# Cross attention in a hybrid layer kernel: the second value product moves ahead of the first operands of w_xo, and two w_xo products move between the heads

## The chip, the cores and the metric

The kernel runs on one core of one Trainium2 chip. The metric is the device time of one execution in microseconds. Five engines work side by side, each through its own queue of instructions in the order in which they were written there: TensorE (PE in the profile; its weight loads are PEld), VectorE (DVE), ScalarE (ACT), GpSimd (POOL) and SyncE (SP), which here only issues the transfers from main memory. An instruction that waits for another engine holds up everything behind it in its own queue.

## The reference, cut to what matters

One layer over 1024 rows of width 1024: a mixer (state space model and causal attention), then a cross attention to 256 memory rows, then a squared-ReLU MLP, each followed by a residual and a layer norm. The change touches the cross attention alone:

```python
def memory_cross_attention(h, mem, w_xq, w_xk, w_xv, w_xo):
    q = (h @ w_xq).reshape(bsz, seq, XATTN_HEADS, XATTN_HEAD_DIM)
    k = (mem @ w_xk).reshape(bsz, m, XATTN_HEADS, XATTN_HEAD_DIM)
    v = (mem @ w_xv).reshape(bsz, m, XATTN_HEADS, XATTN_HEAD_DIM)
    s = jnp.einsum('bshd,bmhd->bhsm', q, k).astype(jnp.float32) * (XATTN_HEAD_DIM ** -0.5)
    p = jax.nn.softmax(s, axis=-1).astype(v.dtype)
    o = jnp.einsum('bhsm,bmhd->bshd', p, v).reshape(bsz, seq, D_MODEL)
    return o @ w_xo
...
h = layer_norm(DN_ALPHA * h + xa, ln2_g[l], ln2_b[l])
```

## The kernel before

**Three matmuls for one.** Operands are split into a rounded high part and a low remainder, and `mm3` (lines 150 to 152) adds hi·hi, hi·lo and lo·hi into one PSUM bank. So each operand costs, ahead of its matmuls, a cast on ACT (the high part) and a subtraction (the low part), most of them on POOL. For weights that is `split_w` (load on SP, cast at line 120, subtraction at line 122). There are four single PSUM banks (names b...) and two double ones (names bb...), taken in turn; a new use of a bank waits until the last use has been read.

**Products of 1024 by 1024** go by Strassen's scheme (`strassen`): seven products, each 48 matmuls of 512 columns on PE, in an order given by a string; for w_xo it is `XOO = '3657142'`. The operands of a product are made by `op_split`: a sum of two quarters takes a copy into a double bank on ACT (line 367), a sum on DVE (line 371), the cast on ACT (line 373) and the subtraction on POOL or DVE (line 375); a single quarter takes the cast on ACT (line 361) and the subtraction on POOL (line 362). `chain` yields such work step by step: each `next` prepares one product's operands or runs one product. The results are added into the residual rows by DVE (line 1192).

**The cross attention** works in eight units: a unit is one half of the rows (hf) and one head (hd), in the order `xu`: (0,0), (0,1), (1,0), (1,1), then the same with heads 2 and 3. A list of short steps, `STEPS`, written by hand, sets their order:

- `k` n: the key product of head n, with two weight tiles of w_xk
- `v` n: the value product, columns 512·n to 512·n+511 of w_xv (two heads), 48 matmuls; `v1` serves heads 2 and 3, units 4 to 7. Four weight tiles go through `split_w`; the two banks are then split into the value tile (cast at line 1357 on ACT, subtraction at line 1358 on DVE)
- `s` n: split of the query of unit n (ACT line 1378, then DVE line 1379), 24 matmuls of 256 columns, row maxima (DVE line 1394), exponentials (ACT line 1397), reciprocals (DVE line 1398) and scaling (POOL line 1401)
- `t` n: eight transposes of the probabilities on PE (line 1409), then the split (ACT line 1411, DVE line 1412)
- `o` n: the value times the probabilities, 12 matmuls of 512 columns; the copies out are line 1422, on ACT and on DVE
- `r`: one of eight residual tiles (ACT line 279, DVE lines 280 and 281)
- `c`: one `next` of the w_xo chain. Product 3 needs units 0, 1 and its weights; product 6 units 0 to 3; product 5 units 0, 1, 4, 5; products 7, 1, 4 and 2 all or some of units 4 to 7

The steps only fix the priority; a scheduler lays the instructions out on each engine's queue in about that order, and the steps of `c` that remain after the list are taken by `norm_between` at line 1504 (13 less the number of `c` in the list). The order on the queues is then fixed in the program.

Of the kernel before, what the change touches and what calls it, by code (L numbers as in the profile page):

```python
# [510 lines left out]
def body(tc, ctx, a, dbg=None):  # L511
# [107 lines left out]
    s5 = k_.slot()  # L619
# [84 lines left out]
    t4 = k_.slot().rearrange("p (g s h) -> p g s h", s=8, h=16)  # L704
# [163 lines left out]
    s4 = [v4(z)[:, :, 0:15, 0:7] for z in sct]  # L868
# [9 lines left out]
    for q in range(2):  # L878
        for two in range(2):
            b = k_.bank()  # L880
            r0 = two * 64
# [475 lines left out]
            A.copy(hi.bitcast(FR), bs[i][:, 0:512])  # L1357
            V.tensor_sub(lo.bitcast(FR), bs[i][:, 0:512], hi)

    STEPS = "k0 s0 k1 s1 t0 r0 v0 r0 t1 o0 s2 r0 k2 o1 r0 s3 t2 r0 k3 o2 r0 t3 s4 r0 o3 c0 r0 v1 t4 s5 o4 s6 c0 t5 o5 c0 t6 s7 o6 c0 t7 o7".split()  # L1360
    steps = [(z[0], int(z[1])) for z in STEPS]

    xq, h1 = {}, {}
# [228 lines left out]
```

## Time and profile before

| | |
|---|---|
| median of 3 runs | 1653.34 us (1650.19 to 1653.36) |
| the profiled execution | 1652.23 us |
| its span, first to last instruction | 1650.4 us |
| mean granted TensorE clock | 0.981 |
| PE busy | 1539.5 us, 93% of the span |
| DVE, POOL, ACT busy | 1243.3, 988.0, 976.5 us (75%, 60%, 59%) |
| the chain that ended last | PE 71%, DVE 15%, ACT 7%, POOL 3%, issue 3% |
| transfers | 71 GB/s mean; queue q1 20.5% of 16 engines |

A row of the timeline has the start, the duration, engine, source line, operation, output and input names, and in brackets the idle time of the engine ahead of it with what ended it. A matmul's duration in a row runs on past the start of the next one, since matmuls are pipelined; the pitch from start to start is what one costs in a row of many. The cross attention from its third transpose on to the fourth w_xo product is the stretch from 844 to 944 us.

### The profile page before, as it was taken

How to read it: one execution, taken by the hardware profiler on the slowest of the kernel's cores; microseconds unless marked ns; L12 is line 12 of the kernel's file. 1: busy time of each engine (PE TensorE's matmuls, PEld its weight loads, DVE VectorE, ACT ScalarE, POOL GpSimd, SP SyncE). 2: the span in 40 equal slices, each digit the busy share in tenths (PEclk: the TensorE clock that was granted, in tenths of full speed). 3: DMA queues.
4: the chain of work that ended last, by engine and by line, in shares of the span. 5: the costliest groups of instructions: out<-in, count | busy, mean ns of one | idle time of the engine just before them, and what ended most of it. 6: DMA issues, size and time to landing. Idle time of an engine off the chain costs nothing.

```text
span 1650.4 us, 20758 instructions
## 1 busy us (share of the span) xinstructions
PE 1539.5 (93%) x7480; PEld 1263.0 (77%) x7480; DVE 1243.3 (75%) x1977; ACT 976.5 (59%) x1415; POOL 988.0 (60%) x538
## 2 busy tenths in 40 slices
PE   6979999999989999999977899899999999999995
PEld 4867778778768778778866687678888888888884
DVE  7970926767777969956574686999598949876998
ACT  5632235666678537684573647766866766667661
POOL 3223243664547767665563554676878767878776
PEclk9989999999999999999998899999999999999998
DMA  6212121111052541103220120022111302021102
GB/s 240 81 39 71 53 71 56 59 60 50 15 177 81 201 154 51 52 0 129 102 102 1 32 86 37 28 75 64 39 51 52 102 1 77 26 103 50 57 22 102
DMA packets 40107, 117.61 MB, mean 71 GB/s; under 512 B 4804, under 2 KB 6340, under 8 KB 40004
## 3 DMA queue, kind: packets, MB, share of 16 engines
q1 hardware_dynamic: 40004, 116.29, 20.5%
q8 instruction: 59, 0.97, 0.2%
q14 instruction: 44, 0.36, 0.1%
HBM read 98.90 MB, written 16.78 MB: 70 GB/s over the span
## 4 chain that ended last, share of the span: by engine, by line
PE 71%; DVE 15%; ACT 7%; POOL 3%; issue 3%; DMA 1%; SPq 0%; POOLq 0%; ACTq 0%; DVEq 0%
PE b L151 20%; PE b L150 20%; PE b L152 20%; DVE sx L1192 1%; PE bb L1034 1%; PE b L1071 1%; DVE c L182 1%; DVE t L371 1%; PE bb L1037 1%; DVE sx L1223 1%; ACT bb L367 1%; PE bb L1038 1%; PE b L1090 1%; DVE sx L224 1%; DVE sa L1249 1%
## 5 line engine op out<-in xcount | busy, mean ns | idle before, releaser
L151 PE MATMUL b<-sw,sa 128*128 128x512 f32 (+3 forms) x1504 | 579.6, 385 | 12.8 <-POOL sw L375 6.7
L150 PE MATMUL b<-sw,sa 128*128 128x512 f32 (+3 forms) x1504 | 578.6, 385 | 12.8 <-ACT sw L120 5.4
L152 PE MATMUL b<-sw,sa 128*128 128x512 f32 (+3 forms) x1504 | 577.7, 384 | 2.7 <-POOL sa L375 2.2
L151 PEld LDWEIGHTS b<-sw,sa 128*128 128x128 f32 x1504 | 284.7, 189 | 71.8 <-POOL sw L375 10.3
L150 PEld LDWEIGHTS b<-sw,sa 128*128 128x128 f32 x1504 | 284.5, 189 | 69.2 <-ACT sw L120 5.7
L152 PEld LDWEIGHTS b<-sw,sa 128*128 128x128 f32 x1504 | 284.5, 189 | 57.9 <-POOL sa L375 4.0
L375 POOL TENSOR_TENSOR sa<-t,sa 128x1024 fp32r<-128x1024 f32 x105 | 257.6, 2469 | 118.8 <-ACT sa L373 106.9
L367 ACT COPY bb<-sa 128x1024 f32<-128x1024 f32 x230 | 233.1, 1018 | 135.8 <-DVE t L371 69.1
L1192 DVE TENSOR_TENSOR sx<-sx,b 128x512 f32<-128x512 f32 x288 | 185.1, 675 | 35.2 <-PE b L152 35.0
L375 POOL TENSOR_TENSOR sw<-t,sw 128x1024 fp32r<-128x1024 f32 x73 | 180.9, 2484 | 43.4 <-ACT sw L373 34.2
L371 DVE TENSOR_TENSOR t<-bb,sa 128x1024 f32<-128x1024 f32 x119 | 144.1, 1217 | 35.1 <-ACT bb L367 18.9
L1249 DVE TENSOR_TENSOR sa<-sa,b 128x512 f32<-128x512 f32 x192 | 124.9, 678 | 46.8 <-ACT sa L1247 33.7
L373 ACT CAST sa<-t 128x1024 fp32r<-128x1024 f32 x105 | 109.1, 1049 | 59.3 <-DVE t L371 58.9
L362 POOL TENSOR_TENSOR sa<-sa,sa 128x1024 fp32r<-128x1024 f32 x36 | 90.2, 2519 | 57.8 <-ACT sa L361 34.2
L122 POOL TENSOR_TENSOR sw<-sraw,sw 128x1024 fp32r<-128x1024 f32 (+4 forms) x28 | 61.9, 2219 | 87.4 <-ACT sw L120 81.8
L150 PE MATMUL b<-sa,sw 128*128 128x512 f32 (+1 forms) x272 | 101.5, 373 | 3.3 <-DVE sa L1249 3.3
L152 PE MATMUL b<-sa,sw 128*128 128x512 f32 (+1 forms) x272 | 99.2, 365 | 0.0
L151 PE MATMUL b<-sa,sw 128*128 128x512 f32 (+1 forms) x272 | 99.2, 365 | 0.0
L362 POOL TENSOR_TENSOR sw<-sa,sw 128x1024 fp32r<-128x1024 f32 x32 | 81.1, 2550 | 27.9 <-ACT sw L361 27.9
L371 DVE TENSOR_TENSOR t<-bb,sraw 128x1024 f32<-128x1024 f32 x53 | 64.2, 1217 | 33.8 <-POOL sw L375 17.8
L373 ACT CAST sw<-t 128x1024 fp32r<-128x1024 f32 x73 | 76.2, 1052 | 15.3 <-PE b L151 7.6
L375 DVE TENSOR_TENSOR sw<-bb,sw 128x1024 fp32r<-128x1024 f32 x47 | 57.2, 1217 | 5.6 <-ACT sw L373 5.5
(341 smaller groups left out, 2792.5 us busy)
## 6 DMA issues: line engine op xcount, KB each, us to landing
sa<-in_w_up_dram SPq DMA_DIRECT2D x24, 512.0 KB, 4.0
sa<-in_w_dn_dram SPq DMA_DIRECT2D x24, 512.0 KB, 4.3
sx<-in_x_dram SPq DMA_DIRECT2D x16, 512.0 KB, 5.8
d_h<-t SPq DMA_DIRECT2D x16, 256.0 KB, 2.3
sraw<-in_w_gs_dram SPq DMA_DIRECT2D x8, 512.0 KB, 3.2
d_gs<-t SPq DMA_DIRECT2D x16, 256.0 KB, 2.9
t<-d_gs SPq DMA_DIRECT2D x16, 256.0 KB, 2.8
d_ms<-t SPq DMA_DIRECT2D x16, 256.0 KB, 2.1
```

Source lines behind the costliest of these rows:

```text
L122: (nc.vector if self.rawtag == "a" and self.nsw % SWV == 0 else nc.gpsimd).tensor_sub(lo[:, :cols].bitcast(FR), raw[:, :cols], hi[:, :cols])
L150: mm(out, A[0].bitcast(FR), B[0].bitcast(FR), start=start, stop=False)
L151: mm(out, A[0].bitcast(FR), B[1].bitcast(FR), start=False, stop=False)
L152: mm(out, A[1].bitcast(FR), B[0].bitcast(FR), start=False, stop=stop)
L182: self.nc.vector.bn_stats(st[:, h, :], x[:, h * 512:(h + 1) * 512])
L362: (GP if z is x[c] else V).tensor_sub(H[c][1].bitcast(FR), z, H[c][0])
L367: A.copy(P[c], x[c])
L371: V.tensor_tensor(T[c], P[c], y[c], op=op)
L373: A.copy(H[c][0].bitcast(FR), T[c])
L375: (V if T[c] is P[c] else GP).tensor_sub(H[c][1].bitcast(FR), T[c], H[c][0])
L1192: V.tensor_tensor(v, v, b, op=op)
L1249: V.tensor_tensor(z[:, s_], z[:, s_], b, op=op)
```

## The change

One string changes: `v1`, one `r`, the `c` steps and some `t` and `s` steps stand in another order, and there are five `c` in the list where there were four.

```diff
-    STEPS = "k0 s0 k1 s1 t0 r0 v0 r0 t1 o0 s2 r0 k2 o1 r0 s3 t2 r0 k3 o2 r0 t3 s4 r0 o3 c0 r0 v1 t4 s5 o4 s6 c0 t5 o5 c0 t6 s7 o6 c0 t7 o7".split()
+    STEPS = "k0 s0 k1 s1 t0 r0 v0 r0 t1 o0 s2 r0 k2 o1 r0 s3 t2 r0 k3 o2 r0 t3 v1 r0 s4 o3 r0 c0 s5 t4 c0 s6 o4 c0 t5 s7 o5 c0 t6 t7 c0 o6 o7".split()
```

The same work is done: the same products, splits, transfers and sums. Up to `t3` the two programs are alike on all engines.

**ACT, from the operands of w_xo's product 3 on to the casts of v1's weights, before.** Names: sa and sw are SBUF tiles (sw the weights' halves), bb a double bank, t a sum. The two L120 rows are the last two weight tiles of `v1`; L1378 is the query of unit 5; the rows to the second L373 are product 3's operands.

```order
L367 COPY bb1518_8069<-sa1504_8045 128x1024
L361 CAST sa1510_8057<-sa1440_7656 128x1024
L367 COPY bb1519_8071<-sa1505_8047 128x1024
L361 CAST sa1512_8059<-sa1461_7790 128x1024
L373 CAST sw1514_8065<-t1520_8073 128x1024
L373 CAST sw1516_8067<-t1521_8075 128x1024
L279 COPY bb1522_8081<-sx1083_5852 128x1024
L1411 CAST sa1532_8156<-b1531_8151 128x512
L1411 CAST sa1534_8164<-b1533_8159 128x512
L120 CAST sw1525_8099<-sa1527_8101 128x1024
L1378 ACTIVATE sa1535_8167<-sa1261_6739 128x1024
L120 CAST sw1528_8117<-sa1530_8119 128x1024
```

The ACT queue of the changed kernel, from the split behind `t3` (the row L1411) on, at the place where those casts stand now; L1378 sa1502 is the query of unit 4, and the two L1357 rows split the finished `v1` banks.

```order
L1411 CAST sa1492_7976<-b1491_7971 128x512
L1378 ACTIVATE sa1502_8049<-sa1257_6707 128x1024
L120 CAST sw1495_7981<-sa1497_7983 128x1024
L120 CAST sw1498_7999<-sa1500_8001 128x1024
L1357 CAST sa1417_7554<-b1493_7979 128x512
L1357 CAST sa1419_7556<-b1494_7980 128x512
L1397 ACTIVATE sa1504_8053,c1506_8067<-bb1505_8054,c1506_8067 128x256 x2
L279 COPY bb1512_8111<-sx1083_5852 128x1024
L1397 ACTIVATE sa1504_8053,c1508_8087<-bb1507_8074,c1508_8087 128x256 x2
```

The two casts of `v1`'s weights stand ahead of unit 4's softmax now; before they stood behind it and behind all of product 3's operands. The split of `v1`'s result has moved up with them.

**ACT, further on in the changed kernel,** from the copy out of `o3` (L1422) on to the split of `t4`'s transposes (the two L1411); the L367, L361 and L373 rows are product 3's operands, L1378 sa1531 the query of unit 5, the two L1397 rows its exponentials.

```order
L1422 COPY sa1509_8094<-b1510_8095 128x512
L367 COPY bb1527_8139<-sa1513_8115 128x1024
L361 CAST sa1519_8127<-sa1440_7656 128x1024
L367 COPY bb1528_8141<-sa1514_8117 128x1024
L361 CAST sa1521_8129<-sa1461_7790 128x1024
L373 CAST sw1523_8135<-t1529_8143 128x1024
L373 CAST sw1525_8137<-t1530_8145 128x1024
L1378 ACTIVATE sa1531_8151<-sa1261_6739 128x1024
L1397 ACTIVATE sa1533_8155,c1535_8169<-bb1534_8156,c1535_8169 128x256 x2
L1411 CAST sa1539_8201<-b1538_8196 128x512
L1397 ACTIVATE sa1533_8155,c1537_8189<-bb1536_8176,c1537_8189 128x256 x2
L1411 CAST sa1541_8209<-b1540_8204 128x512
```

Before, L1378 of unit 5 and the split of `t4` (the L1411 rows) stood behind product 3's operands as well; but between `t4` and unit 5's scores PE had the second half of `v1`. Now `v1` is done by then, and the split of `t4` stands behind L1378 and between the exponentials of unit 5.

**PE, the transposes of the last units, before:** the names ending in 8503 and 8511 are the banks of `t7`, 8520 and 8528 those of `o7`.

```order
L1409 MATMUL b1605_8503<-cst_58,sa1584_8418 128x128
L1409 MATMUL b1607_8511<-cst_58,sa1584_8418 128x128
L150 MATMUL b1610_8520<-sa1606_8508,sa1417_7554 128x512
L150 MATMUL b1611_8528<-sa1606_8508,sa1417_7554 128x512
L151 MATMUL b1610_8520<-sa1606_8508,sa1417_7554 128x512
```

PE at that place in the changed kernel: 8470 and 8478 are the banks of `t6`, 8486 and 8494 those of `t7`, 8502 the first bank of w_xo's product 6.

```order
L1409 MATMUL b1598_8470<-cst_58,sa1559_8247 128x128 x4
L1409 MATMUL b1600_8478<-cst_58,sa1559_8247 128x128 x4
L1409 MATMUL b1602_8486<-cst_58,sa1577_8385 128x128 x2
L1409 MATMUL b1604_8494<-cst_58,sa1577_8385 128x128 x2
L1409 MATMUL b1602_8486<-cst_58,sa1577_8385 128x128
L1409 MATMUL b1604_8494<-cst_58,sa1577_8385 128x128
L1409 MATMUL b1602_8486<-cst_58,sa1577_8385 128x128
L1409 MATMUL b1604_8494<-cst_58,sa1577_8385 128x128
L150 MATMUL b1606_8502<-sw1549_8227,sa1542_8212 128x512
L151 MATMUL b1606_8502<-sw1550_8228,sa1542_8212 128x512
L152 MATMUL b1606_8502<-sw1549_8227,sa1543_8213 128x512
```

The 48 matmuls of product 6 now stand ahead of both `o6` and `o7`, and `t6` and `t7` stand together and take all four single banks; b1606 is the bank that b1598 had.

On SP the loads of `v1`'s last two weight tiles move ahead of four loads of w_xo. The two come into tiles that the scores of unit 3 free (before: into tiles that the split of `t3` and unit 4's scores free).

## Rows read from the trace of the kernel before

**Rows 1.** The page: TensorE's busy time with its share of the span, and the clock granted to it in 40 equal slices of 41.3 us (in tenths of full speed; 21 and 22 are the slices from 866 to 949 us).

```profile
PE 1539.5 (93%) x7480; PEld 1263.0 (77%) x7480; DVE 1243.3 (75%) x1977; ACT 976.5 (59%) x1415; POOL 988.0 (60%) x538
PEclk9989999999999999999998899999999999999998
```

**Rows 2.** Busy time by stage. Columns: the stretch and its length, then for PE, PEld, DVE, ACT and POOL the busy us with the number of instructions, then the granted clock as a share of full speed, the transfers' share and GB/s. The first is the whole stretch that the change reorders, the next three are parts of it, the last lies behind it.

```profile
844.45:943.46 99.01, 73.26 (x333) 57.85 (x333) 55.77 (x69) 53.77 (x88) 46.15 (x33) 0.84 0.12 42
857.90:876.90 19.00, 9.18 (x25) 6.83 (x26) 6.84 (x7) 7.86 (x10) 13.09 (x6) 0.64 0.00 0
887.30:899.70 12.40, 5.04 (x13) 3.57 (x14) 7.97 (x10) 10.85 (x19) 7.65 (x7) 0.72 0.00 0
922.60:932.60 10.00, 5.65 (x12) 4.01 (x13) 5.17 (x6) 7.36 (x10) 2.65 (x2) 0.51 0.00 1
943.70:996.00 52.30, 52.30 (x236) 43.12 (x235) 44.38 (x82) 26.66 (x33) 28.57 (x13) 1.00 0.24 81
```

**Rows 3.** The timeline of PE: the end of `t4`'s transposes, the first matmuls behind the long waits (of `v1`'s second half twice, of `o5`, of `o7`), and the first matmul of w_xo's product 5.

```profile
856.85 1.03 PE L1409 MATMUL b<-cst,sa 128*128 128x128 f32 x8
863.33 1.22 PE L150 MATMUL b<-sw,sa 128*128 128x512 f32 x2 [5.44 <-ACT sw L120]
868.94 0.79 PE L151 MATMUL b<-sw,sa 128*128 128x512 f32 x1 [4.39 <-POOL sw L122]
894.27 1.22 PE L150 MATMUL b<-sa,sa 128*128 128x512 f32 x2 [7.07 <-ACT sa L1411]
926.55 1.22 PE L150 MATMUL b<-sa,sa 128*128 128x512 f32 x2 [4.00 <-ACT sa L1411]
943.68 0.39 PE L150 MATMUL b<-sw,sa 128*128 128x512 f32 x1
```

**Rows 4.** The timeline of PE, pitches: first and last of 24 matmuls of 512 columns (`v1`'s first half), of 12 in `v1`'s second half, and of 24 of 256 columns (unit 5's scores).

```profile
851.40 0.39 PE L150 MATMUL b<-sw,sa 128*128 128x512 f32 x1
856.62 0.39 PE L152 MATMUL b<-sw,sa 128*128 128x512 f32 x1
...
869.96 0.63 PE L150 MATMUL b<-sw,sa 128*128 128x512 f32 x1
874.65 0.53 PE L150 MATMUL b<-sw,sa 128*128 128x512 f32 x1
...
876.84 0.28 PE L150 MATMUL bb<-sa,sa 128*128 128x256 f32 x1
879.59 0.28 PE L152 MATMUL bb<-sa,sa 128*128 128x256 f32 x1
```

**Rows 5.** The loads of `v1`'s last two weight tiles: their issue on the SP queue; their size and median us from issue to landing in the list of transfers from 830 to 1000 us; and, of the timeline of PE, the last matmul of unit 3's scores.

```profile
851.12 0.83 SPq L119 DMA_DIRECT2D sa<-in_w_xv_dram  x2
sa<-in_w_xv_dram SPq DMA_DIRECT2D x4, 512.0 KB, 4.2
835.75 0.28 PE L152 MATMUL bb<-sa,sa 128*128 128x256 f32 x1
```

**Rows 6.** The timeline of ACT: the query of unit 4, then from the residual tile behind unit 4's exponentials on (a copy, casts of product 3's operands, the query of unit 5).

```profile
845.01 1.07 ACT L1378 ACTIVATE sa<-sa 128x1024 fp32r<-128x1024 f32 x1
...
852.94 1.04 ACT L279 COPY bb<-sx 128x1024 f32<-128x1024 f32 x1
853.88 1.04 ACT L367 COPY bb<-sa 128x1024 f32<-128x1024 f32 x1
854.82 1.08 ACT L361 CAST sa<-sa 128x1024 fp32r<-128x1024 f32 x1
...
858.44 1.99 ACT L373 CAST sw<-t 128x1024 fp32r<-128x1024 f32 x2
...
863.18 1.06 ACT L1378 ACTIVATE sa<-sa 128x1024 fp32r<-128x1024 f32 x1
```

**Rows 7.** The timeline of POOL: subtractions for `v1`'s weight tiles, the first two and the last two.

```profile
842.33 4.74 POOL L122 TENSOR_TENSOR sw<-sa,sw 128x1024 fp32r<-128x1024 f32 x2 [3.09 <-PE b L152]
...
865.56 5.65 POOL L122 TENSOR_TENSOR sw<-sa,sw 128x1024 fp32r<-128x1024 f32 x2
```

**Rows 8.** The timeline of DVE: the low half of the query (line 1379) of units 5, 6 and 7; and of POOL, the subtractions that run beside the last of them.

```profile
864.84 1.86 DVE L1379 SCALAR_TENSOR_TENSOR sa<-sa,sa 128x1024 fp32r<-128x1024 f32 x1
883.27 1.21 DVE L1379 SCALAR_TENSOR_TENSOR sa<-sa,sa 128x1024 fp32r<-128x1024 f32 x1
913.50 2.58 DVE L1379 SCALAR_TENSOR_TENSOR sa<-sa,sa 128x1024 fp32r<-128x1024 f32 x1 [0.16 <-ACT sa L1378]
910.26 4.74 POOL L362 TENSOR_TENSOR sw<-sraw,sw 128x1024 fp32r<-128x1024 f32 x2 [9.26 <-ACT sw L361]
```

**Rows 9.** The timeline around the last units: of PE the last matmul of product 3, the first of `o6` and the last transposes of `t7`; of ACT the last cast of product 5's operands ahead of the split of `t7`; of DVE the subtraction behind it and the split itself.

```profile
910.29 0.39 PE L152 MATMUL b<-sw,sa 128*128 128x512 f32 x1
912.07 0.73 PE L150 MATMUL b<-sa,sa 128*128 128x512 f32 x2 [0.52 <-ACT sa L1411]
921.66 0.89 PE L1409 MATMUL b<-cst,sa 128*128 128x128 f32 x4 [0.50 <-POOL sa L1401]
925.01 1.00 ACT L373 CAST sa<-bb 128x1024 fp32r<-128x1024 f32 x1
926.30 1.22 DVE L375 TENSOR_TENSOR sa<-bb,sa 128x1024 fp32r<-128x1024 f32 x1
927.43 1.28 DVE L1412 TENSOR_TENSOR sa<-b,sa 128x512 fp32r<-128x512 f32 x2
```

## The prediction

> **What bounds the kernel now.** I read the page first: TensorE is busy for 93% of the span and its clock is full in almost every slice, but the slices from 866 to 949 us show 0.8 [rows 1]. Then the stages: between the end of `t3`'s transposes (844.45) and product 5's first matmul (943.68, 99.2 us) PE is busy for only 73.3 us at a mean clock of 0.84, and in the 52.3 us behind it all the time at full clock [rows 2]. So the stretch that the change reorders is bound by waits, and its surroundings by PE. Third, PE's timeline names the waits: 5.44 and 4.39 us for the cast and the subtraction of `v1`'s last weights, 7.07 for the split of `t5`, 4.00 for the split of `t7` [rows 3]. Each also costs clock: behind the second wait twelve matmuls start 0.426 us apart (869.96 to 874.65, the 1.2 GHz level), against 0.227 in `v1`'s first half and 0.120 for 256 columns [rows 4].
>
> The work in the stretch by full-clock pitches: 204 matmuls of 512 columns (`v1` 48, `o3` to `o7` 60, products 3 and 6 96) 46.3 us, 96 of 256 columns 11.5, 32 transposes about 3.5 (eight take 1.03 with their tail) [rows 3]. That is 61.3, so 37.9 us are waits and low clock. That is the most the change can give.
>
> **The change part by part.** I lay the new order out from 844.45, each engine in its queue's order.
>
> *`v1` early.* Its loads went out at 851.12 and take about 4.2 us, because their tiles were freed late; the new tiles are free when unit 3's scores end at 836 [rows 5]. So the data is there by about 841. ACT casts it right behind unit 4's query (845.01 for 1.07, one copy later now, so to about 846.6) [rows 6]: casts at 846.6 and 847.5. POOL finishes the first two tiles at 847.1 (842.33 + 4.74) [rows 7], then subtracts at half of 4.74 each: low halves at 849.9 and 852.3. PE needs them after 24 and 36 matmuls, at 849.9 and 852.6. So both long `v1` waits go and nothing takes their place: 48 × 0.227 = 10.9, to 855.5. If the loads were late after all, each microsecond would be one here.
>
> *Unit 4's scores and `o3`:* 24 × 0.12 + 12 × 0.227 = 5.6, to 861.1; `t4` with 0.4 wait for its scaling, to 862.4.
>
> *Unit 5's scores.* Their query split (L1378) stands on ACT behind product 3's operands. Unit 4's exponentials end about 2 us behind its scores (851.0 to 852.94 before) [rows 4, 6], now 860.6 with the residual copy between them. Then a half copy of 0.5, two L367, two L361, two L373 at 0.95 each (pitch 853.88 to 854.82) [rows 6]: 866.8; L1378 gives the high half at 867.8. PE waits 5.4 us: this is the old 5.44 come back at another place. What hid it before was `v1`'s second half, and that cover is gone.
>
> The low half (L1379, DVE) took 1.21, 1.86 and 2.58 us; the long one started while POOL's subtractions ran until 915.0 (910.26 + 4.74), and 915.0 plus 1.1 is its end [rows 8]. Now it falls among POOL's four subtractions for product 3, so it takes 1.2 at best and a whole subtraction more, 3.6, at worst; I take 2.6, to 870.4.
>
> The Trainium skill says in "SBUF — State Buffer", section "Who interferes with whom", that a DVE instruction with two SBUF inputs and a GpSimd instruction that reads SBUF exclude each other for a whole instruction, the later one waiting. The 2.58 us row agrees: it is a wait of 1.5 and then the usual 1.1. By the rule POOL has the port nearly all of this time; if its subtraction has just begun the term is 3.6 and the sum below 12.2; if DVE comes first, the term is 1.2 and the sum 14.6. The row's 2.6 gives 13.2.
>
> Then 20 matmuls at the low clock, about 0.21 each (half of 0.426, an estimate): 4.3, to 874.7.
>
> *`o4`.* The split of `t4` stands between unit 5's two exponentials, so its second half is done only after scores, maximum 0.7, exponentials 0.95, cast and subtraction 1.2: about 877.9. PE gets some ten matmuls in and loses about 2 us.
>
> *First half of product 3, `s6`, second half, `t5`.* Four matmuls of `o4` and 22 of product 3 are left ahead of `s6`: 26 × 0.227 = 5.9, and 2 more if ten are still at the low clock: 7.9, to 885.8. Unit 6's query is ready at about 884.9 (five steps of product 6's preparation at 0.95 stand ahead of it on ACT, and POOL pauses), so no wait. Then `s6` takes 3.1 and the second half 5.4: product 3 ends at 894.4, with `t5` (0.9) behind it. The 7.07 us wait for `t5`'s split has gone: product 3 and unit 6 cover it.
>
> *`o5`, unit 7, `t6`, `t7`.* These follow product 3 as `o6`, unit 7 and `t7` did: 912.07 is 1.55 behind the end of product 3 (910.29 + 0.23), so 895.95 now. Before, `t7`'s last transposes ended 10.5 us after 912.07 (921.66 + 0.89) [rows 9]; `t6` fits into its wait: 906.4.
>
> *Product 6 takes over `o7`'s wait.* It needs a bank, and all four hold `t6` and `t7`; their split stands behind five steps of product 5's operands on ACT. Before, the last such cast ended at 926.0, the DVE subtraction behind it takes 1.13 and the first split 0.65 [rows 9]: 927.8, that is 15.7 behind 912.07, now 911.7. PE waits 5.3 us. Product 6 takes 48 × 0.227 = 10.9 and about 2.4 for twelve matmuls at the low clock; `o6` and `o7` 24 × 0.227 = 5.4. Product 5 starts at 930.5.
>
> **The sum:** 943.7 − 930.5 = 13.2 us. Of 37.9 us lost before, about 24.7 stay: 5.4 + 1.8 at unit 5, 2 at `o4`, 2 for small waits ahead of `o5` and in unit 7, 1.7 ahead of `t7`, 5.3 ahead of product 6, and 6 of low clock. Against the profiled execution, 1652.2 − 13.2 = 1639.0 us. The median of the runs lies 1.1 above that execution, which I leave in the range. The ends of the unknown terms: L1379 at 1.2 with the clock back up by `o4`, −2.6; L1379 at 3.6 with all 26 matmuls low, +3.4. So the forecast's own range is 1635.5 to 1643.5.
>
> **The rivals.**
>
> 1. *The clock stays low.* Unit 5's start, L1379 and `o4` give three waits in a row where before there was one long wait and then dense work. If PE stays at 1.2 GHz until unit 6's scores end, 16 matmuls more at 0.2 and 24 at 0.1 are added, 5.6 us: 1644.6. For it: the stretch from 887.3 to 899.7 has a mean of 0.72 with only two waits [rows 2]. Against it: behind the 4.39 us wait PE resumed at 868.94, and at 876.84 the pitch was the full one [rows 3, 4]. The Trainium skill's "TensorE: Matmul & The Clock Gate", section "A second HAM failure mode: psum-queue depth-cycling", describes a TensorE that idles shortly between groups of matmuls and swings between the two levels; by that this rival is what happens.
>
> 2. *Part is given back behind product 5.* Product 7 needs `o6` and `o7`. Between `o7` and it stood products 6 and 5 (21.8 us), now product 5 alone (10.9). From `o7`'s end I count 7.7 us to its last operand (copy out, two sums, then three POOL subtractions of 2.4), so 3 us to spare. For it: DVE is busy for 44.4 of the 52.3 us behind 943.7 [rows 2], and five sums of 1.14 that it did ahead of product 5 now come behind its start, 5.7 us more; for product 1 I count about 1 us to spare. If both products are 2 us late with 2.5 of low clock each, 9 us come back: 1648. Against it: 44.4 + 5.7 is still below 52.3.
>
> 3. *Slower, by the same mechanism all the way.* If the operands of products 7, 1, 4 and 2 each take over 14 us from one product's start to the next's (four subtractions of 2.4 and 4.4 of waits in the queue between ACT, DVE and POOL), PE idles 3.4 us and loses 2.9 of clock four times: 25 us, 1664. It decides from 10.9 + 3.3 us on per product. Four subtractions alone are 9.6, which speaks against it.
>
> 4. *The wait only moves.* If unit 5's start and product 6's bank come some 5 us later each, since ACT or DVE wait inside product 3's and 5's operands, the gain is 3 us or less: 1650.
>
> 5. *Better:* with L1379 short, and the clock up throughout, all 6 us of low clock go as well: 1633.
>
> **How the numbers follow.** Forecast 0.60, rival 1 0.10, rival 2 0.12, rival 3 0.05, rival 4 0.05, rival 5 0.08. The range 1634 to 1647 leaves out rivals 3 and 4, half of 2 and half of 5: 0.20. No change is what lies within 0.2% (3.3 us), about what a measurement of this kernel tells apart. Faster: forecast, rivals 1 and 5, half of 2: 0.84. Within: rival 4 and half of 2: 0.11. Slower: rival 3, 0.05.
>
> **What would show it.** In the changed profile: no PE wait on L120 or L122 behind 844 us; `v1` ending near 855.5; a PE wait of about 5.4 us on L1378 ahead of unit 5's scores; no 7 us wait ahead of `o5`; a wait of about 5 us on L1412 ahead of product 6; product 5 starting near 930.5 and no wait behind it up to 980. The prediction is wrong if `v1` waits for its loads, if product 6 doesn't wait for a bank, or if products 7 and 1 wait for their operands.

## The result, and the profile after

| | before | after |
|---|---|---|
| median of 4 runs each, on one chip | 1653.01 us | 1640.37 us (1638.41 to 1641.91) |
| ratio, with its 95% interval | | 0.9925 (0.9913 to 0.9938) |
| the profiled execution and its span | 1652.23, 1650.4 us | 1638.41, 1636.6 us |
| a second set of runs of both | 1652.9 us | 1640.68 us, 0.9924 (0.9909 to 0.9939) |

The kernel is 12.6 us faster by the medians. The page of the changed kernel, TensorE's busy time and its granted clock, answers to [rows 1]:

```profile
PE 1534.9 (94%) x7480; PEld 1260.5 (77%) x7480; DVE 1243.0 (76%) x1977; ACT 976.3 (60%) x1415; POOL 990.0 (60%) x538
PEclk9989999999999999999998999999999999999998
```

It says almost nothing: the work is the same, the busy times nearly so, and of the two neighbouring slices at 0.8 in the middle one is left. The stages say more. Busy time by stage after the change, with the columns of [rows 2]: the time up to product 5, the first nine matmuls of product 6, and the 52.3 us behind product 5's start.

```profile
844.45:930.68 86.23, 69.69 (x336) 56.05 (x333) 51.17 (x65) 44.95 (x80) 40.72 (x30) 0.90 0.11 37
912.38:916.38 4.00, 4.00 (x9) 3.14 (x10) 1.74 (x3) 0.96 (x2) 0.00 (x0) 0.50 0.00 0
930.68:983.00 52.32, 52.32 (x236) 43.10 (x235) 49.23 (x85) 34.98 (x42) 35.70 (x15) 1.00 0.23 81
```

The first row of [rows 2] had 73.3 us of PE busy in 99.0 at a clock of 0.84; here it is 69.7 in 86.2 at 0.90. PE is idle for 16.5 us instead of 25.8, and busy for 3.6 us less with the same matmuls, which is the clock. In the 52.3 us behind product 5's start PE is busy all the time and at full clock, as it was before.

PE's timeline after the change: the start of `t3`'s transposes, then the waits up to product 6 (without some of under 1 us) with the last matmuls of `v1` (856.33) and of product 3 (894.71) between them, the start of product 5, the first wait behind that, and the first matmul of the MLP's first product, behind the norm.

```profile
843.65 1.03 PE L1409 MATMUL b<-cst,sa 128*128 128x128 f32 x8
851.43 0.50 PE L151 MATMUL b<-sw,sa 128*128 128x512 f32 x1 [0.36 <-POOL sw L122]
856.33 0.39 PE L152 MATMUL b<-sw,sa 128*128 128x512 f32 x1
868.97 0.58 PE L150 MATMUL bb<-sa,sa 128*128 128x256 f32 x1 [5.26 <-ACT sa L1378]
872.39 0.58 PE L152 MATMUL bb<-sa,sa 128*128 128x256 f32 x1 [2.20 <-DVE sa L1379]
877.21 0.73 PE L150 MATMUL b<-sa,sa 128*128 128x512 f32 x2 [0.84 <-ACT sa L1411]
894.71 0.40 PE L152 MATMUL b<-sw,sa 128*128 128x512 f32 x1
896.54 0.73 PE L150 MATMUL b<-sa,sa 128*128 128x512 f32 x2 [0.57 <-ACT sa L1411]
912.38 0.79 PE L150 MATMUL b<-sw,sa 128*128 128x512 f32 x1 [5.35 <-DVE sa L1412]
930.68 0.39 PE L150 MATMUL b<-sw,sa 128*128 128x512 f32 x1
1001.49 0.44 PE L332 MATMUL bb<-cst,sx 128*128 128x128 f32 x2 [0.53 <-ACT sx L222]
1007.22 0.50 PE L150 MATMUL b<-sw,sa 128*128 128x512 f32 x1 [0.28 <-ACT sa L1247]
```

The waits of [rows 3] (5.44 and 4.39 us inside `v1`, 7.07 ahead of `o5`, 4.00 ahead of `o7`) are gone. In their place stand 5.26 us for unit 5's query (line 1378), 2.20 for its low half (line 1379) and 5.35 for a bank ahead of product 6 (line 1412). The same two end points in the trace of before are:

```profile
843.42 1.03 PE L1409 MATMUL b<-cst,sa 128*128 128x128 f32 x8
1021.42 0.50 PE L150 MATMUL b<-sw,sa 128*128 128x512 f32 x1 [0.28 <-ACT sa L1247]
```

From the first of `t3`'s transposes to that matmul of line 150 it took 178.0 us before and takes 163.6 now. I use this length, read from the same two rows of every trace and called the stretch from here on, beside the medians: it holds all that the step list reorders, and leaves out the differences between executions that arise elsewhere. In the repeated profile of the changed kernel it was 164.8, so two executions of one kernel can differ by 1.2 us here; most of that is how long the clock stayed low behind two of the waits, as shown further on.

### The profile page after: what moved, and what is told of

The parts are those of the page before. It is cut to its first block, busy times and chain, and to the rows that moved or that the text cites. A ratio compares the mean times of both kernels' runs of the same rounds, so it can differ in the third digit from the quotient of the medians.

```text
span 1636.6 us, 20760 instructions
## 1 busy us (share of the span) xinstructions
PE 1534.9 (94%) x7480; PEld 1260.5 (77%) x7480; DVE 1243.0 (76%) x1977; ACT 976.3 (60%) x1415; POOL 990.0 (60%) x538
## 4 chain that ended last, share of the span: by engine, by line
PE 68%; DVE 16%; ACT 7%; POOL 4%; issue 3%; DMA 1%; SPq 0%; POOLq 0%; ACTq 0%; DVEq 0%
PE b L150 20%; PE b L152 19%; PE b L151 19%; DVE sx L1192 1%; POOL sa L375 1%; DVE c L182 1%; DVE t L371 1%; POOL sw L375 1%; PE b L1071 1%; PE bb L1034 1%; DVE sx L1223 1%; PE bb L1037 1%; ACT bb L367 1%; ACT sa L373 1%; PE bb L1038 1%
## 5 line engine op out<-in xcount | busy, mean ns | idle before, releaser
L367 ACT COPY bb<-sa 128x1024 f32<-128x1024 f32 x230 | 233.1, 1018 | 125.4 <-DVE t L371 61.0
L373 ACT CAST sa<-t 128x1024 fp32r<-128x1024 f32 x105 | 109.1, 1049 | 59.0 <-DVE t L371 58.6
L373 ACT CAST sw<-t 128x1024 fp32r<-128x1024 f32 x73 | 76.3, 1053 | 15.7 <-PE b L151 7.8
```

Of the source, the lines that this page charges most:

```text
L367: A.copy(P[c], x[c])
L373: A.copy(H[c][0].bitcast(FR), T[c])
```

## The experiments

All of them change only the list `STEPS`, from `t3` on. The diffs show only that part of the list, those of e2, e3, e4, e5 and e9 against the changed kernel, the others against the kernel named beside them. In it the `c` steps are, in order: product 3's operands, product 6's operands, product 3, product 5's operands, product 6.

| run | change | median us | ratio to before (95%) | the stretch us |
|---|---|---|---|---|
| before | | 1653.0 | 1 | 178.0 |
| after, twice | | 1640.4, 1640.7 | 0.9925 (0.9913 to 0.9938), 0.9924 (0.9909 to 0.9939) | 163.6, 164.8 |
| e1 | `v1` alone moved | 1650.7 | 0.9990 (0.9982 to 0.9999) | 175.1 |
| e2, twice | all of the change but `v1`'s move | 1637.6, 1637.9 | 0.9908 (0.9893 to 0.9922), 0.9901 (0.9887 to 0.9914) | 163.2, 163.1 |
| e3 | `s5` ahead of product 3's operands | 1638.4 | 0.9917 (0.9902 to 0.9931) | 164.1 |
| e4 | product 5's operands behind `t7` | 1632.7 | 0.9877 (0.9863 to 0.9890) | 156.8 |
| e5, twice | `t7` behind product 6 | 1632.4, 1630.6 | 0.9875 (0.9859 to 0.9890), 0.9858 (0.9844 to 0.9871) | 155.5, 155.5 |
| e8 | e5, `v1` behind `s4` | 1630.3 | 0.9864 (0.9849 to 0.9879) | 153.8 |
| e9, twice | e2 with e5 | 1629.0, 1628.8 | 0.9860 (0.9843 to 0.9876), 0.9847 (0.9834 to 0.9861) | 153.4, 152.8 |
| e10 | e9, `s5` ahead of `v1` and of product 3's operands | 1632.3 | 0.9865 (0.9849 to 0.9880) | 155.4 |

My theory was that the gain comes from the order of the products among the heads, since product 3 now covers the split of `t5`, and that `v1`'s move only exchanges one wait for another. The first rival was that `v1` carries the gain; its two waits are, after all, the ones that the trace of before shows first. For the waits that remain the theory was that each is the end of ACT's queue, put down to whatever stands last in it; the rival, that each can be removed by moving the one instruction that PE waits for.

**e1: `v1` alone.** Against the kernel before:

```diff
-t3 s4 r0 o3 c0 r0 v1 t4 s5 o4 s6 c0 t5 o5 c0 t6 s7 o6 c0 t7 o7
+t3 v1 s4 r0 o3 c0 r0 t4 s5 o4 s6 c0 t5 o5 c0 t6 s7 o6 c0 t7 o7
```

> The kernel before with `v1` alone put ahead of unit 4's scores; product 3's operands, unit 5, unit 6 and the other `c`s stand as before. My theory: the move of `v1` gains little by itself. The two waits for `v1`'s last weights (5.44 and 4.39 us) go, but unit 5's query split then waits on ACT behind product 3's operands as it does in the changed kernel, and the 7.07 us wait for the split of `t5` stays, since nothing of product 3 stands ahead of it. I expect 1 to 4 us less than before, 1649 to 1652, with a wait of 4 to 6 us on L1378 or L1411 ahead of unit 5 or `o4`, and a wait of 6 to 8 us ahead of `o5`. The rival, that `v1` carries the gain: 9 us or more, 1644 or less, and no wait of over 3 us between `v1` and `o4`.

It took 1650.7 us against 1652.7 on the same chip, 2.0 us less, with an interval that nearly reaches no change. PE's timeline shows the two waits that the theory named, ahead of `o4` and ahead of `o5`:

```profile
870.74 1.22 PE L150 MATMUL b<-sa,sa 128*128 128x512 f32 x2 [5.73 <-ACT sa L1411]
893.45 1.22 PE L150 MATMUL b<-sa,sa 128*128 128x512 f32 x2 [7.07 <-ACT sa L1411]
```

Nearly 10 us of waits inside `v1` were removed and 2 us came of it. 5.7 us came straight back a few steps on, and the wait ahead of `o5` is the 7.07 us of [rows 3] to the hundredth.

**e2: everything but `v1`'s move,** against the changed kernel. The `c` steps stand in the new order, and so do the `s` and `t` steps between them (unit 7's scores ahead of `o5`, `t6` and `t7` together):

```diff
-t3 v1 r0 s4 o3 r0 c0 s5 t4 c0 s6 o4 c0 t5 s7 o5 c0 t6 t7 c0 o6 o7
+t3 s4 r0 o3 r0 c0 v1 s5 t4 c0 s6 o4 c0 t5 s7 o5 c0 t6 t7 c0 o6 o7
```

> The changed kernel with `v1` put back behind product 3's operands, so that only the order of the products' operands and products among the heads is new. My theory: this part carries most of the gain. Product 3 covers the split of `t5`, so the 7.07 us wait ahead of `o5` goes, while one or both waits for `v1`'s last weights stay. I expect 10 to 13 us less than before, 1640 to 1643, a wait of 3 to 6 us on L120 or L122 inside `v1`, and no wait of over 2 us ahead of `o5`. The rival, that `v1` carries the gain: 4 us or less, 1649 or more.

It took 15.1 us less than before on the same chip, more than the whole change does and more than the 10 to 13 that I expected. Its PE timeline: the first and last matmul of `v1`'s first half, then the waits ahead of unit 5's scores, inside `v1`'s second half, ahead of `o5` and ahead of product 6:

```profile
854.24 0.39 PE L150 MATMUL b<-sw,sa 128*128 128x512 f32 x1
859.47 0.39 PE L152 MATMUL b<-sw,sa 128*128 128x512 f32 x1
863.57 0.39 PE L150 MATMUL bb<-sa,sa 128*128 128x256 f32 x1 [2.83 <-ACT sa L1378]
871.87 0.79 PE L151 MATMUL b<-sw,sa 128*128 128x512 f32 x1 [2.47 <-POOL sw L122]
898.51 0.73 PE L150 MATMUL b<-sa,sa 128*128 128x512 f32 x2 [0.52 <-ACT sa L1411]
914.31 0.79 PE L150 MATMUL b<-sw,sa 128*128 128x512 f32 x1 [5.30 <-DVE sa L1412]
```

The wait inside `v1` is 2.47 us, less than the 3 to 6 of the expectation. The 7.07 us wait ahead of `o5` is 0.52 with `v1` late, so it is the new order of the other steps that removes it, and the first rival has fallen. No run moves the `c` steps without the `s` and `t` steps, so that it is product 3's place is read from the traces alone: before, five steps of product 6's operands stood on ACT ahead of the split of `t5` (887.9 to 893.6 us) while PE had nothing to do; in the changed kernel they run beside product 3 (from 878.5 on), and the split, at 895.9, follows the transposes at once. That `v1` late is even a little better I had not expected, so both e2 and its twin further on were run again:

> The kernel with `v1` late and the products' operands in the new order, once more, to settle the sign of `v1`'s part: the first time it took 0.9908 of before, the changed kernel 0.9925 and 0.9924. If `v1` early costs 1 to 3 us on top of the rest, this comes out at 0.990 to 0.9915 again; if the two are equal, at 0.992 to 0.993.

It came out at 0.9901, the stretch again at 163.1. By the medians `v1` early costs some 3 us on top of the new order, with intervals that overlap; the stretch shows 0.4 to 1.7 of it. The rows show why it doesn't help: with `v1` late its first half (854.24 to 859.7, 5.5 us) runs on PE while ACT begins product 3's operands, and unit 5's query costs 2.83 us instead of 5.26, which pays for the 2.47 on line 122. A second cause may work beside this: on e2's ACT queue unit 5's query stands ahead of the last two casts of product 3's operands, where in the changed kernel it stands behind them. No run separates the two.

```profile
862.47 1.05 ACT L1378 ACTIVATE sa<-sa 128x1024 fp32r<-128x1024 f32 x1
863.42 1.98 ACT L373 CAST sw<-t 128x1024 fp32r<-128x1024 f32 x2
```

**e3: unit 5's scores ahead of product 3's operands.**

```diff
-t3 v1 r0 s4 o3 r0 c0 s5 t4 c0 s6 o4 c0 t5 s7 o5 c0 t6 t7 c0 o6 o7
+t3 v1 r0 s4 o3 r0 s5 c0 t4 c0 s6 o4 c0 t5 s7 o5 c0 t6 t7 c0 o6 o7
```

> The changed kernel with unit 5's scores put ahead of product 3's operands in the order of steps, so that L1378 no longer stands behind them on ACT. My theory: ACT's queue between `v1` and `o4` is the limit, not the place of one instruction in it. The 5.26 us wait on L1378 goes, the casts of `t4` (L1411) then stand behind product 3's operands, and a wait of 5 to 9 us appears ahead of `o4`: the time of the changed kernel within 2 us. The rival, that the wait at unit 5's query split is the loss itself: no such wait comes up, and the kernel takes 6 to 9 us less, 1631 to 1634.

The ratio is 0.9917 beside 0.9924 for the changed kernel on the same chip, the stretch 164.1 beside 164.8: no change that can be told. PE's timeline, unit 5's low half and `o4`, and of DVE the low half itself:

```profile
864.72 0.38 PE L152 MATMUL bb<-sa,sa 128*128 128x256 f32 x1 [0.99 <-DVE sa L1379]
875.35 0.79 PE L150 MATMUL b<-sa,sa 128*128 128x512 f32 x1 [7.98 <-ACT sa L1411]
863.45 1.22 DVE L1379 SCALAR_TENSOR_TENSOR sa<-sa,sa 128x1024 fp32r<-128x1024 f32 x1
```

The wait on line 1378 is gone, and 7.98 us stand ahead of `o4` instead, for the split of `t4`, which is now what is last behind product 3's operands. The rival (6 to 9 us less) has fallen: moving the one instruction that PE waits for moves the wait. This run also measures line 1379 apart from the rest, 1.22 us where the changed kernel took 3.39; I come back to that below.

**e4 and e5: the bank ahead of product 6,** in two ways, product 5's operands behind `t7` or `t7` behind product 6.

```diff
-t3 v1 r0 s4 o3 r0 c0 s5 t4 c0 s6 o4 c0 t5 s7 o5 c0 t6 t7 c0 o6 o7
+t3 v1 r0 s4 o3 r0 c0 s5 t4 c0 s6 o4 c0 t5 s7 o5 t6 t7 c0 c0 o6 o7
```

```diff
-t3 v1 r0 s4 o3 r0 c0 s5 t4 c0 s6 o4 c0 t5 s7 o5 c0 t6 t7 c0 o6 o7
+t3 v1 r0 s4 o3 r0 c0 s5 t4 c0 s6 o4 c0 t5 s7 o5 c0 t6 c0 t7 o6 o7
```

> The changed kernel with product 5's operands put behind `t7` instead of ahead of `t6`. In the changed kernel product 6 waits 5.35 us for a bank, because the casts of `t6` and `t7` (L1411) stand on ACT behind five steps of product 5's operands. My theory: without these steps ahead of them the casts run directly behind unit 7's exponentials, product 6 starts some 5 us earlier and without its 1.9 us of low clock: about 7 us less than the changed kernel, 1633 to 1635. The first rival: product 5's operands then come too late and the same wait of about 5 us stands ahead of product 5 or 7, so the time is that of the changed kernel, 1640 within 1.5. The second rival: the wait ahead of product 6 is for its own operands, not for the bank; then product 6 starts no earlier.

> The changed kernel with `t7` put behind product 6 in the order of steps; product 5's operands stay where they are. My theory is the bank: product 6 then finds two banks that `o5` left, starts at about 904.7 instead of 912.4, and waits some 2 us at its third bank, which `t6` holds until its split is done. That is about 5 us less than the changed kernel, near 1635. The rival, that product 6 waits for its operands or that ACT's queue alone sets the end of the stretch: product 6 still begins near 912, or the same wait stands ahead of `o6` or `o7`, and the time is that of the changed kernel within 1.5 us.

They took 1632.7 and 1632.4 us, 0.3 under the range given for e4 and 2.6 under the 1635 given for e5. PE's timeline of e4: the last of `t7`'s transposes and the first matmul of product 6.

```profile
909.76 0.89 PE L1409 MATMUL b<-cst,sa 128*128 128x128 f32 x4 [0.38 <-POOL sa L1401]
910.40 0.49 PE L150 MATMUL b<-sw,sa 128*128 128x512 f32 x1
```

And of e5: `t6`'s transposes, product 6's first matmul, and product 5's first.

```profile
908.11 1.03 PE L1409 MATMUL b<-cst,sa 128*128 128x128 f32 x8
908.89 0.48 PE L150 MATMUL b<-sw,sa 128*128 128x512 f32 x1
926.21 0.39 PE L150 MATMUL b<-sw,sa 128*128 128x512 f32 x1
```

In both, product 6 starts right behind the transposes and at the full pitch, so its operands were there all along and the wait was for the bank. Both rivals of e4 have fallen, and that of e5: no wait comes back ahead of product 5. The stretch is 6.8 and 8.1 us shorter than in the first profile after the change, 8.0 and 9.3 shorter than in the second. In e5 I had expected 2 us of wait at product 6's third bank, and so a gain of 5 us; PE has no wait anywhere in that product, though `t6`'s split was not done until 917.6. That miss is in my count of the banks.

**e9: the two gains together,** `v1` late and `t7` behind product 6.

```diff
-t3 v1 r0 s4 o3 r0 c0 s5 t4 c0 s6 o4 c0 t5 s7 o5 c0 t6 t7 c0 o6 o7
+t3 s4 r0 o3 r0 c0 v1 s5 t4 c0 s6 o4 c0 t5 s7 o5 c0 t6 c0 t7 o6 o7
```

> Two earlier runs put together: `v1` behind product 3's operands, as before the change, and `t7` behind product 6. If `v1`'s move adds nothing on top of the order of the products, this has the time of the run with `t7` behind product 6 alone, 1632, within 2 us, and its waits are the 2.8 us on L1378 and the 2.5 us on L122 in place of the 5.3 and 2.2 us on L1378 and L1379. The rival, that `v1` early is worth some 3 us also here: 1635 or more.

1629.0 us and a stretch of 153.4, 2.1 less than e5; the median is 1 us under what I gave it (1632 within 2), and the rival (1635 or more) has fallen. The waits are the two that were named, the one inside `v1` 0.8 us longer than in e2:

```profile
859.48 0.39 PE L150 MATMUL bb<-sa,sa 128*128 128x256 f32 x1 [2.84 <-ACT sa L1378]
867.77 0.79 PE L151 MATMUL b<-sw,sa 128*128 128x512 f32 x1 [3.29 <-POOL sw L122]
```

To settle the sign, e5 and e9 were run once more side by side:

> The changed kernel with `t7` behind product 6, once more, beside its twin with `v1` late, for the same question. If `v1` early costs 1 to 3 us on top of the rest, this is 1 to 3 us behind the twin; if not, the two agree within 1 us. I expect 1632.

> `v1` late and `t7` behind product 6, once more, beside its twin with `v1` early. I expect 1629 to 1630, 1 to 3 us ahead of the twin.

1630.6 and 1628.8 us, the stretch 155.5 and 152.8. The medians are 3.4 and 1.7 us apart, the stretches 2.1 and 2.7, always with the same sign, but the intervals of the medians overlap both times. So `v1` early gains 2 to 3 us by itself and, as far as this tells, costs 1 to 3 on top of the new order. By the medians e9 is the fastest kernel of this study, 24 to 25 us ahead of before; the interval of e8, below, overlaps with its own.

**e8 and e10: `v1` or unit 5 elsewhere,** both with `t7` behind product 6. Against e9:

```diff
-t3 s4 r0 o3 r0 c0 v1 s5 t4 c0 s6 o4 c0 t5 s7 o5 c0 t6 c0 t7 o6 o7
+t3 r0 s4 v1 r0 o3 c0 s5 t4 c0 s6 o4 c0 t5 s7 o5 c0 t6 c0 t7 o6 o7
```

```diff
-t3 s4 r0 o3 r0 c0 v1 s5 t4 c0 s6 o4 c0 t5 s7 o5 c0 t6 c0 t7 o6 o7
+t3 s4 r0 o3 r0 s5 v1 c0 t4 c0 s6 o4 c0 t5 s7 o5 c0 t6 c0 t7 o6 o7
```

> `v1` between unit 4's scores and `o3`, so that its 10.9 us on PE cover unit 4's exponentials and product 3's operands on ACT, and `t7` behind product 6. My theory says that unit 5's wait is product 3's operands in ACT's queue with nothing long on PE beside them: ACT is idle for 6.6 us beside `v1` in the changed kernel, and here the operands stand in that time. The waits on L1378 and L1379 (5.3 and 2.2 us) go or shrink below 2 us in all, and with the 1.5 us of low clock behind them the kernel takes 6 to 9 us less than with `t7` moved alone: 1623 to 1626. The rival: `v1`'s last weights, whose loads may go out late again since unit 4's tiles are taken first, wait on L120 or L122 inside `v1` for 3 us or more, and the time is 1629 or more.

> Unit 5's scores ahead of both `v1` and product 3's operands, `t7` behind product 6. ACT then forms unit 5's query right behind unit 4's exponentials while PE is in `v1`'s first half, so the wait on L1378 goes. My theory, that ACT's queue holds up whatever stands last in it, says that the casts of `v1`'s last weights, now behind unit 5's exponentials, are what PE waits for: 3 to 6 us on L120 or L122 inside `v1`, and the time of the run with `v1` late and `t7` behind product 6 (1629) within 2 us. The rival, that the stretch has room in ACT's queue and only this order was missing: no wait of over 2 us up to `o4`, and 1625 or less.

e8 missed: 1630.3 where I expected 1623 to 1626. Its timeline, PE inside `v1` and at unit 5's two halves, and of ACT the split of `v1`'s result:

```profile
861.29 0.50 PE L151 MATMUL b<-sw,sa 128*128 128x512 f32 x1 [1.43 <-POOL sw L122]
870.17 0.38 PE L150 MATMUL bb<-sa,sa 128*128 128x256 f32 x1 [3.27 <-ACT sa L1378]
872.68 0.58 PE L152 MATMUL bb<-sa,sa 128*128 128x256 f32 x1 [1.75 <-DVE sa L1379]
865.25 0.59 ACT L1357 CAST sa<-b 128x512 fp32r<-128x512 f32 x1 [2.76 <-PE b L152]
```

The rival's time came out, but not by its mechanism, since the wait inside `v1` is only 1.43 us. What I had left out is that the scheduler puts the split of `v1`'s result (line 1357) between product 3's operands on ACT, and ACT stood idle for 2.76 us until `v1` was done, with the rest of the operands and unit 5's query behind it. No run moves that split, so this is read from the rows alone.

e10 gave the waits that the theory asked for, ahead of `v1`'s second half and inside it, and one more ahead of `o4`:

```profile
867.52 0.73 PE L150 MATMUL b<-sw,sa 128*128 128x512 f32 x2 [2.83 <-ACT sw L120]
870.14 0.80 PE L151 MATMUL b<-sw,sa 128*128 128x512 f32 x1 [1.88 <-POOL sw L122]
879.04 0.73 PE L150 MATMUL b<-sa,sa 128*128 128x512 f32 x2 [2.18 <-ACT sa L1411]
```

At 1632.3 us it is 1.3 us outside what I gave it (1629 within 2), which the third wait would account for; the rival (1625 or less) has fallen. The changed kernel run again was to show how far sets of runs differ:

> The changed kernel itself, once more, beside the three that follow: a measure of how far a kernel's time moves from one set of runs to the next. I expect 12 to 13 us less than before, 1639 to 1641.

1640.7 against 1652.9.

## Why the prediction was right

The forecast was 1639.0 us; the profiled execution took 1638.4, the medians 1640.4 and 1640.7. Product 5 starts 13.2 us earlier from `t3` on (943.68 less 843.42 is 100.3, 930.68 less 843.65 is 87.0), which is the forecast's sum. That it is met to the tenth is luck: in the repeated profile of the same kernel product 5 starts 12.0 us earlier (88.3 us behind `t3`), and in the first one errors cancel, as told below. 1.2 us more come at the norm in both. Step by step:

- **`v1` early: right.** No wait on line 120, 0.36 us on line 122; the loads' issue stands at 830.70 now, 20 us before [rows 5]. `v1`'s last matmul starts at 856.33, so it ends about 1 us behind the 855.5 that I had. POOL's pair of subtractions took 5.76 us, not 4.74; its row stands below.
- **Unit 5's query: right,** 5.26 us for 5.4, at 868.97 for 867.8.
- **Its low half: mis-sized,** 3.39 us for the 2.6 I took, close to the upper end of 3.6. PE went on at 872.39 for 870.4.
- **The low clock behind it: in part mis-sized.** I took 20 matmuls at 0.21 and about ten of `o4` at twice their full pitch. The low pitch is right (872.77 to 875.12, 11 steps, 0.214), but in this execution it ends inside the scores, and `o4` is back at the full 0.23:

```profile
872.77 0.42 PE L150 MATMUL bb<-sa,sa 128*128 128x256 f32 x1
875.12 0.41 PE L151 MATMUL bb<-sa,sa 128*128 128x256 f32 x1
878.50 0.40 PE L151 MATMUL b<-sa,sa 128*128 128x512 f32 x1
880.41 0.39 PE L152 MATMUL b<-sa,sa 128*128 128x512 f32 x1
```

  In the repeated profile of the same kernel, as in those of e4, e5 (both) and e8, it holds through all 20 of the scores, as I had it; there it is `o4`'s ten that were too many. Of the repeated profile, the second and the last of the 20 at the low pitch (871.27 to 875.11, 18 steps, 0.213), and the last of the matmuls at the low pitch behind the bank ahead of product 6:

```profile
871.27 0.41 PE L150 MATMUL bb<-sa,sa 128*128 128x256 f32 x1
875.11 0.41 PE L152 MATMUL bb<-sa,sa 128*128 128x256 f32 x1
916.40 0.58 PE L152 MATMUL b<-sw,sa 128*128 128x512 f32 x1
```

- **`o4`:** 0.84 us of wait for about 2. The errors of the last four steps nearly cancel, which is luck: product 3's last matmul starts at 894.71 and ends 0.5 us behind the 894.4 that I had.
- **`o5` without its 7 us wait: right** (0.57 us, started at 896.54 for 895.95). e1 and e2 show that it does not hang on `v1` but on the order of the other steps.
- **Product 6 waits for a bank: right,** 5.35 us for 5.3, at 912.38 for 911.7, and e4 and e5 show that it is the bank. The low clock behind it took nine matmuls (912.38 to 916.38, 4.0 us, 2.0 more than at 0.227) for the twelve and 2.4 us of the forecast; in the repeated profile it took twelve (911.54 to 916.82, 2.6 us more).

The rivals: the clock did not stay low up to unit 6's scores, in either profile of the changed kernel (1). Nothing was given back behind product 5 (2, 3): PE has no wait there until 1001.49, and DVE is busy for 49.2 of the 52.3 us, close to the 50.1 by which I argued. The waits did move, but their sum fell (4). The better case (5) needed a short low half, which didn't come.

What the working did not say is which part of the change does it. It laid out one order and counted 37.9 us of loss before and 24.7 after (the terms that it lists add up to 24.2), and so credited `v1`'s two waits along with `o5`'s. By e1 and e2 the gain belongs to the new order of the `c`, `s` and `t` steps, and by the medians `v1` would have been better left.

The price of line 1379 is told by two rows that start 0.05 us apart, POOL's subtractions and DVE's low half, in the changed kernel; then by the pair of POOL beside unit 4's low half:

```profile
868.90 5.66 POOL L375 TENSOR_TENSOR sw<-t,sw 128x1024 fp32r<-128x1024 f32 x2
868.95 3.39 DVE L1379 SCALAR_TENSOR_TENSOR sa<-sa,sa 128x1024 fp32r<-128x1024 f32 x1 [2.59 <-ACT sa L1378]
...
847.91 1.21 DVE L1379 SCALAR_TENSOR_TENSOR sa<-sa,sa 128x1024 fp32r<-128x1024 f32 x1
847.96 5.76 POOL L122 TENSOR_TENSOR sw<-sa,sw 128x1024 fp32r<-128x1024 f32 x2 [0.45 <-ACT sw L120]
```

Where POOL is first by 0.05 us, DVE takes 3.39; where DVE is first by 0.05 us, it takes 1.21. In both the pair on POOL takes about 1 us more than the 4.74 of [rows 7], about the time of one DVE instruction in between. The Trainium skill says in "SBUF — State Buffer", section "Who interferes with whom", that the two exclude each other for a whole instruction; the rows agree, here at nearly the full price of one subtraction. Values in between come as well, the 1.86 and 2.58 of [rows 8] and, in e8, 2.48, where POOL had begun 0.98 us before:

```profile
869.17 5.69 POOL L375 TENSOR_TENSOR sw<-t,sw 128x1024 fp32r<-128x1024 f32 x2
870.15 2.48 DVE L1379 SCALAR_TENSOR_TENSOR sa<-sa,sa 128x1024 fp32r<-128x1024 f32 x1 [2.16 <-ACT sa L1378]
```

So DVE waits out what is left of POOL's subtraction, and the term hangs on where in it DVE's instruction falls. The 2.6 that I took belongs to a start some 0.9 us into one; here POOL's had just begun, which the prediction named as its upper end.

## What to carry to other kernels

A wait that the profile shows first is not the one that is worth most: ask what the waiting engine's supplier does next, and undo each part of a change alone before crediting it. Where a queue (here ACT between `v1` and `o4`) is late as a whole, moving the instruction that is waited for only moves the wait; what helped was long work on PE set beside the late queue, and a step that holds banks put behind the product that needs them. Transposes whose split comes late should not take all the banks just ahead of a long product.

## What the runs showed of the hardware

- Whether DVE or POOL was first by 0.05 us decided about 2.2 us on DVE (3.39 against 1.21), with the same outcome in both profiles of the changed kernel (3.39 and 3.37). With POOL's subtraction begun 0.98 us before, it was 2.48.
- A wait of 5.35 us cost more than itself: removed in e5, it gave 8.1 us by the stretch, of which 2.0 are the low clock of the nine matmuls behind it (a granted clock of 0.50 there, the 1.2 GHz level); against the second profile it gave 9.3, of which 2.6 are the low clock. The rest, about 1 us, is no more than two profiles of one kernel differ by.
- Behind one and the same wait (5.30 to 5.36 us, ahead of product 6) the low clock held for 9 to 13 matmuls in five profiles: nine and twelve in those of the changed kernel, ten in both of e2, thirteen in e3.
- `t3` started between 841.9 and 847.3 us in the profiles of this study, although the steps ahead of it are the same in all; these two ends are the two profiles of one program, e5. Its cause wasn't tried; it is why the stretch, not the span, was compared.
